# Low parts of the weights: ScalarE's negated high part and an adding DMA from GpSimd, in place of a VectorE subtraction

## The chip, the cores and the metric
The kernel runs on one core of one Trainium2 chip. The metric is the device time of one execution in microseconds (us). The engines have short names in the profile: PE is TensorE (PEld its weight loads), DVE VectorE, ACT ScalarE, POOL GpSimd, and SP the engine that issues DMAs and computes nothing.

## What is computed
One layer of a hybrid decoder, for a prompt of 2048 positions and for 8 sample positions that share the weights:

```
shift, scale, gate = split(silu(c) @ w_ada + b_ada)
h    = x * (1 + scale) + shift
u_s, z_s, q, k, v, z_a, g_s, g_a = split(h @ w_in)
b_s  = (GLU(gelu(SSM(u_s)), w_glu) * silu(z_s)) @ w_branch_s
b_a  = (attention(q, k, v) * silu(z_a)) @ w_branch_a
m    = sigmoid(g_s) * b_s + sigmoid(g_a) * b_a
y    = layer_norm(alpha * x + gate * (m @ w_out))
```

The model width is 1024, all data are float32, and the states and the K/V caches are outputs too.

## The kernel before
**Products from three parts.** The matrix products run in the type float32r, which holds fewer bits than float32. So each operand is split into a high part (the value rounded to float32r) and a low part (value minus high part), and a product is the sum of three: high by high, low of the activations by high of the weights, and high by low of the weights. chunk_k (L75 to L78) issues the three for one slice k of 128 rows; whi and wlo are the two parts of a weight, hh and hl (later xh and xl) those of the activations. chunk (L65) does the 8 slices into one PSUM tile acc (3 buffers), and products (L80) goes over jobs: a job is one weight of 1024 x 128, used for 5 chunks of positions (512, 256, 512, 264 and 512 columns), each with an evacuation evac of its own behind it.

**Where a weight comes from.** split_w (L49 to L60) loads it into the tile wst (one buffer, SP's queue, L55), ScalarE rounds it to whi (L58), and VectorE subtracts to wlo (L59). whi and wlo have two buffers each, so the next weight's parts can be written when TensorE has finished the weight before the present one. products calls split_w for the next weight after the second chunk of the present one; but the order on each engine is made by a scheduler, which puts every instruction where its own model of the times has it, and is then fixed. An engine takes its instructions strictly in that order. 74 weights pass through split_w; w_out and the V projection have code of their own.

**The stages.** At the start (phase_in, L108) the weights of the modulation are loaded and multiplied (ada, L183 to L191), the activations are transposed (L228), scaled to hh (ScalarE, L235) and split to hl (L240: VectorE, and GpSimd for three slices of eight), and the first two weights are split, whose first chunk fills TensorE between the modulation matmuls. Then come the products of w_in, first beside the preparation of the state-space tables, then beside the state-space pairs (ssm_pairs, L684; about 335 to 920 us), in which GpSimd makes small pieces: dg (L763), which VectorE adds into kt (L768), and copies into S (L799 to L806). Attention runs beside further products of w_in (to about 1495 us). Phase 4 has the GLU product (about 1585 to 1780 us), branch a and branch s. In the GLU stage each chunk's evacuation (L1187 to L1196) loads a stored chunk z, ScalarE takes its sigmoid zs and the sigmoid sg of acc, GpSimd multiplies zs by z (L1192) and adds the two parts of the activations into z (L1193), VectorE multiplies twice (L1194, L1195), and SP stores. Last is the product with w_out and the layer norm.

Of the kernel before, what the change touches and what calls it, by code (L numbers as in the profile page):

```python
# [9 lines left out]
F32 = mybir.dt.float32  # L10
F32R = mybir.dt.float32r
I32 = mybir.dt.int32
AF = mybir.ActivationFunctionType
OP = mybir.AluOpType
# [25 lines left out]
class Trunk:  # L40
# [8 lines left out]
    def split_w(self, parts, st=None):  # L49

        nc = self.nc
        if st is None:
            st = self.wp.tile([128, KT, 128], F32, name="wst", bufs=1)
        for src, dst in parts:
            nc.sync.dma_start(dst(st), src)  # L55
        hi = self.wp.tile([128, KT, 128], F32R, name="whi")
        lo = self.wp.tile([128, KT, 128], F32R, name="wlo")
        nc.scalar.copy(hi, st)  # L58
        nc.vector.tensor_tensor(lo, st, hi, op=OP.subtract)  # L59
        return hi, lo  # L60

    def cols(self, w, c0):
# [1333 lines left out]
```

## Time and profile before
| what | value |
|---|---|
| time of the runs shown | 2338.59 us, median of 2 (2336.45 and 2340.74) |
| the profiled execution | 2341.11 us, of which the span of the trace is 2339.3 us |
| busy: PE, DVE, ACT, POOL | 2274.6, 1393.7, 755.1, 329.1 us |
| granted TensorE clock, mean | 0.995 of full speed |
| DMA queue of SP | 388,576 packets, 315.8 MB, 47% of what 16 DMA engines could be busy |
| HBM read and written | 195.3 MB and 122.6 MB |

Busy times are sums over the span; an engine can be busy for little and still be waited for. Every DMA of this kernel is issued by SP. The end of a matmul is modelled, since matmuls are pipelined: the distance from one start to the next tells more than a duration.

### The profile page before, as it was taken

The page shows a single profiled execution, that of the slowest core. Times are in us where ns is not written, and L with a number is a line of the kernel's source. Part 1 is how long each engine was busy: PE and PEld are TensorE (multiplying, and loading weights), DVE is VectorE, ACT ScalarE, POOL GpSimd, SP SyncE. Part 2 cuts the span into 40 slices and gives each one's busy share as a digit, 9 for nine tenths or more (in the row PEclk, how much of TensorE's full clock was granted, in tenths as well). Part 3 has the DMA queues.
Part 4 walks back from the last instruction along what each step waited for, and adds up shares of the span by engine and source line. Part 5 has one row for each costly group of instructions (what it writes and reads, how often), then busy time and mean ns, then how long its engine had stood idle before and what let it go on. Part 6 is the DMA issues. An engine that isn't in the chain of part 4 may idle for free. (4 is left out here: it accounts for less than half of the span.)

```text
span 2339.3 us, 35133 instructions
## 1 busy us (share of the span) xinstructions
PE 2274.6 (97%) x12819; PEld 1903.5 (81%) x12819; DVE 1393.7 (60%) x3100; ACT 755.1 (32%) x1636; POOL 329.1 (14%) x412
## 2 busy tenths in 40 slices
PE   7999999999999999899999999999998999999998
PEld 5888898788888888677888888887877888888886
DVE  4896229888888872067776666426436214224887
ACT  3411213331111211166665565435224113212100
POOL 1100001111101100000010000013542000222232
PEclk9999999999999999999999999999999999999999
DMA  9344623344434445443343333448337546767431
GB/s 290 101 150 127 209 69 112 111 117 119 120 111 121 115 110 127 93 131 111 110 137 96 108 100 114 108 114 221 112 104 231 154 124 198 218 179 230 150 120 65
DMA packets 388749, 318.02 MB, mean 136 GB/s; under 512 B 90582, under 2 KB 332654, under 8 KB 386991
## 3 DMA queue, kind: packets, MB, share of 16 engines
q1 hardware_dynamic: 388576, 315.78, 47.0%
q8 instruction: 101, 1.65, 0.3%
q14 instruction: 72, 0.59, 0.1%
HBM read 195.28 MB, written 122.63 MB: 136 GB/s over the span
## 5 line engine op out<-in xcount | busy, mean ns | idle before, releaser
L78 PE MATMUL acc<-hh,whi 128*128 128x512 f32 (+2 forms) x2000 | 714.0, 358 | 11.2 <-ACT zr L582 10.7
L78 PE MATMUL acc<-hl,whi 128*128 128x512 f32 (+2 forms) x2000 | 706.7, 353 | 0.0
L78 PE MATMUL acc<-hh,wlo 128*128 128x512 f32 (+2 forms) x2000 | 703.2, 352 | 0.0
L78 PEld LDWEIGHTS acc<-hh,whi 128*128 128x128 f32 x2000 | 378.3, 189 | 64.8 <-ACT zr L582 11.1
L78 PEld LDWEIGHTS acc<-hl,whi 128*128 128x128 f32 x2000 | 378.6, 189 | 53.1 <-issue 7.6
L78 PEld LDWEIGHTS acc<-hh,wlo 128*128 128x128 f32 x2000 | 378.1, 189 | 53.1 <-issue 6.9
L78 PE MATMUL acc<-xh,whi 128*128 128x512 f32 (+2 forms) x960 | 336.5, 351 | 15.1 <-ACT sg L1190 13.3
L78 PE MATMUL acc<-xl,whi 128*128 128x512 f32 (+2 forms) x960 | 335.5, 349 | 3.0 <-DVE xl L1138 2.9
L78 PE MATMUL acc<-xh,wlo 128*128 128x512 f32 (+2 forms) x960 | 333.7, 348 | 0.0
L78 PEld LDWEIGHTS acc<-xh,whi 128*128 128x128 f32 x960 | 181.5, 189 | 43.5 <-ACT sg L1190 17.8
L78 PEld LDWEIGHTS acc<-xl,whi 128*128 128x128 f32 x960 | 181.7, 189 | 27.7 <-DVE xl L1138 5.4
L78 PEld LDWEIGHTS acc<-xh,wlo 128*128 128x128 f32 x960 | 181.5, 189 | 23.0
L1138 DVE TENSOR_TENSOR xl<-xst,xh 128x1024 fp32r<-128x1024 f32 (+2 forms) x84 | 105.7, 1275 | 81.0 <-ACT xh L1137 80.0
L59 DVE TENSOR_TENSOR wlo<-wst,whi 128x1024 fp32r<-128x1024 f32 x74 | 95.6, 1292 | 93.0 <-ACT whi L58 92.3
L1035 DVE SCALAR_TENSOR_TENSOR t<-ps,bias 128x512 f32<-128x512 f32 (+1 forms) x128 | 82.7, 671 | 97.7 <-PE ps L1033 96.4
L872 ACT ACTIVATE t<-t,nm 128x256 f32<-128x256 f32 (+1 forms) x256 | 125.5, 492 | 45.2 <-DVE es L869 29.1
L58 ACT CAST whi<-wst 128x1024 fp32r<-128x1024 f32 x74 | 77.6, 1049 | 149.2 <-PE acc L78 146.2
L1137 ACT CAST xh<-xst 128x1024 fp32r<-128x1024 f32 (+2 forms) x84 | 86.0, 1043 | 106.7 <-DMA xst<-mD 34.1
L1068 POOL TENSOR_TENSOR o<-o,z 128x512 f32<-128x512 f32 x32 | 42.6, 1330 | 548.3 <-ACT o L1067 533.2
L582 ACT COPY zr<-acc 128x512 f32<-128x512 f32 (+2 forms) x120 | 60.0, 500 | 168.0 <-PE acc L78 70.5
L1330 PE MATMUL po<-wol,xh 128*128 128x512 f32 (+1 forms) x272 | 102.8, 378 | 0.8 <-DVE wol L1253 0.8
L1330 PE MATMUL po<-woh,xh 128*128 128x512 f32 (+1 forms) x272 | 102.8, 378 | 0.1
(354 smaller groups left out, 3259.8 us busy)
## 6 DMA issues: line engine op xcount, KB each, us to landing
wst<-in_w_in SPq DMA_DIRECT2D x50, 512.0 KB
uD<-u SPq DMA_DIRECT2D x8, 1088.0 KB
u<-uD SPq DMA_DIRECT2D x32, 272.0 KB
yD<-y SPq DMA_DIRECT2D x64, 132.0 KB
x<-in_x_prompt SPq DMA_DIRECT2D x16, 512.0 KB
wa<-in_w_ada SPq DMA_DIRECT2D x16, 512.0 KB
qf<-qD SPq DMA_DIRECT2D x32, 256.0 KB
z<-zaP SPq DMA_DIRECT2D x32, 256.0 KB
```

The costliest lines, as they stand in the source:

```text
L58: nc.scalar.copy(hi, st)
L59: nc.vector.tensor_tensor(lo, st, hi, op=OP.subtract)
L78: self.nc.tensor.matmul(ps[:, :n], w[:, k, :], x[:, k, :], start=(k == 0 and i == 0), stop=(k == KT - 1 and i == 2))
L582: nc.scalar.copy(z[:, :n], ps[:, :n])
L872: nc.scalar.activation(t1[:, h, kw], t1[:, h, kw], AF.Exp, bias=nm[:, h:h + 1], accum_out=den[:, h:h + 1])
L1035: v.scalar_tensor_tensor(t1[:, 2 * g:2 * g + 2, kw], ps[:, :, kw], 0.125, s["bias"][:, hd, b0:b0 + kw.stop], op0=OP.mult, op1=OP.add)
L1068: nc.gpsimd.tensor_tensor(o4, o4, s["z4"], op=OP.mult)
L1137: nc.scalar.copy(xv(hi[:, k - 1:k + 1]), sv(st))
L1138: nc.vector.tensor_tensor(xv(lo[:, k - 1:k + 1]), sv(st), xv(hi[:, k - 1:k + 1]), op=OP.subtract)
L1330: nc.tensor.matmul(ps[:, :w], X[a][:, k, ts], Wo[h * w // 512][b][:, k, ws], start=(i == 0), stop=(i == 23))
```

## The change
One statement of split_w goes and two come. ScalarE writes the negated high part into wlo, and a DMA issued by GpSimd adds the weight, read from HBM once more, to what stands in wlo: st - hi as before, computed as -hi + st.

```diff
         nc.scalar.copy(hi, st)
-        nc.vector.tensor_tensor(lo, st, hi, op=OP.subtract)
+        nc.scalar.activation(lo, hi.bitcast(F32), AF.Copy, scale=-1.0)
+        for src, dst in parts:
+            nc.gpsimd.dma_start(dst(lo), src, accum_op=OP.add)
         return hi, lo
```

Lines behind L59 stand two further down in the changed kernel (L240 becomes L242, L78 becomes L80). The scheduler orders all engines anew. Three places follow.

GpSimd at the start, before: the subtractions for hl of the first chunks stand one behind the other.

```order
L240 TENSOR_TENSOR hl_197<-h,hh_196 128x512 x3
L240 TENSOR_TENSOR hl_506<-h,hh_505 128x256 x3
L240 TENSOR_TENSOR hl_621<-h,hh_620 128x512 x3
L240 TENSOR_TENSOR hl_729<-h,hh_728 128x256 x3
L240 TENSOR_TENSOR hl_833<-h,hh_832 128x512 x3
```

The same place now (L61 is the adding DMA):

```order
L242 TENSOR_TENSOR hl_197<-h,hh_196 128x512
L61 DMA wlo<-in_w_in 128x8x128 x2
L242 TENSOR_TENSOR hl_197<-h,hh_196 128x512 x2
L242 TENSOR_TENSOR hl_508<-h,hh_507 128x256 x3
L242 TENSOR_TENSOR hl_623<-h,hh_622 128x512 x3
L242 TENSOR_TENSOR hl_731<-h,hh_730 128x256 x3
```

The DMAs for the first two weights stand between the first and the second hl of the first chunk.

TensorE at the start, before (pm is the modulation's sum, md and x are transposed, acc the product of the first weights):

```order
L78 MATMUL acc<-hh_196,whi 128x512
L188 MATMUL tr<-ident,md 128x128
L183 MATMUL pm<-wa,c_182 32x128
L78 MATMUL acc<-hl_197,whi 128x512
L78 MATMUL acc<-hh_196,wlo 128x512
L183 MATMUL pm<-wa,c_182 32x128 x15
L228 MATMUL tr<-ident,x 128x128 x4
L78 MATMUL acc<-hh_196,whi 128x512
L188 MATMUL tr<-ident,md 128x128
L183 MATMUL pm<-wa,c_182 32x128
```

TensorE now, from the last modulation matmuls on:

```order
L185 MATMUL pm<-wa,c_182 32x128 x16
L190 MATMUL tr<-ident,md 128x128
L185 MATMUL pm<-wa,c_182 32x128 x16
L190 MATMUL tr<-ident,md 128x128
L230 MATMUL tr<-ident,x 128x128 x6
L80 MATMUL acc<-hh_507,whi 128x256
L230 MATMUL tr<-ident,x 128x128 x6
L80 MATMUL acc<-hh_196,wlo 128x512
L80 MATMUL acc<-hh_196,whi 128x512
L80 MATMUL acc<-hl_197,whi 128x512
```

The first matmul that reads wlo stood among the modulation matmuls and now stands behind the last of them. Before that last one, 30 large matmuls (10 of them on wlo) stand in the order of before, and 4 (none on wlo) in that of the change.

GpSimd in the GLU stage, before, over one change of weight (zs and z of the chunks of 264, 512, 512 and 256 columns):

```order
L1192 TENSOR_TENSOR zs_17003<-zs_17003,z_17001 128x264
L1193 TENSOR_TENSOR z_17001<-xh4_16052,xl4_16053 128x264
L1192 TENSOR_TENSOR zs_17039<-zs_17039,z_17037 128x512
L1193 TENSOR_TENSOR z_17037<-xh2_16002,xl2_16003 128x512
L1192 TENSOR_TENSOR zs_17075<-zs_17075,z_17073 128x512
L1193 TENSOR_TENSOR z_17073<-xh0_15700,xl0_15701 128x512
L1192 TENSOR_TENSOR zs_17111<-zs_17111,z_17109 128x256
```

GpSimd in the GLU stage now, from the chunk of 256 columns on:

```order
L1194 TENSOR_TENSOR zs_16980<-zs_16980,z_16978 128x256
L1195 TENSOR_TENSOR z_16978<-xh3_15996,xl3_15997 128x256
L61 DMA wlo_16992<-in_w_glu 128x8x128
L1194 TENSOR_TENSOR zs_17023<-zs_17023,z_17021 128x512
L1195 TENSOR_TENSOR z_17021<-xh1_15946,xl1_15947 128x512
L1194 TENSOR_TENSOR zs_17059<-zs_17059,z_17057 128x264
```

The sequence of zs and z is the old one; one DMA stands in it per weight, behind the z of the 256-column chunk.

## Rows read from the trace of the kernel before

**Rows 1.** The page's part 1: busy us, share of the span, instructions.
```profile
PE 2274.6 (97%) x12819; PEld 1903.5 (81%) x12819; DVE 1393.7 (60%) x3100; ACT 755.1 (32%) x1636; POOL 329.1 (14%) x412
```

**Rows 2.** Windows: stretch, its us, each engine's busy us, PEclk, DMA share, GB/s.
```profile
20.00:47.00 27.00, 22.07 (x253) 14.54 (x252) 11.41 (x34) 8.48 (x16) 2.12 (x2) 1.00 1.17 301
47.00:100.00 53.00, 52.03 (x326) 43.98 (x325) 45.15 (x135) 33.37 (x61) 14.93 (x15) 1.00 0.42 140
...
335.00:920.00 585.00, 578.24 (x3099) 486.05 (x3098) 469.57 (x990) 132.88 (x239) 69.78 (x186) 1.00 0.41 116
...
1585.00:1780.00 195.00, 183.78 (x966) 155.04 (x965) 97.12 (x106) 71.33 (x108) 87.17 (x73) 1.00 0.52 147
```

**Rows 3.** Waits of TensorE: for whom, us in total, times, longest.
```profile
PE acc L78 <- ACT sg L1190: 13.3, 15, 3.6
```

**Rows 4.** Timeline, ScalarE and TensorE, branch a: start, us, engine line op.
```profile
1852.95 1.06 ACT L58 CAST whi<-wst 128x1024 fp32r<-128x1024 f32 x1
...
1875.33 0.39 PE L78 MATMUL acc<-xl,whi 128*128 128x512 f32 x1
1875.56 0.39 PE L78 MATMUL acc<-xh,wlo 128*128 128x512 f32 x1
```

**Rows 5.** Timeline, ScalarE, GpSimd and TensorE, GLU stage, one weight.
```profile
1662.18 1.03 ACT L58 CAST whi<-wst 128x1024 fp32r<-128x1024 f32 x1
1663.12 1.26 ACT L1190 ACTIVATE sg<-acc,bglu 128x512 f32<-128x512 f32 x2
...
1664.46 1.06 POOL L1193 TENSOR_TENSOR z<-xh,xl 128x256 f32<-128x256 f32 x1
1673.21 1.29 POOL L1192 TENSOR_TENSOR zs<-zs,z 128x512 f32<-128x512 f32 x1 [7.69 <-ACT zs L1191]
...
1680.53 0.39 PE L78 MATMUL acc<-xh,wlo 128*128 128x512 f32 x1
```

**Rows 6.** Groups by line: shapes, count, busy us, mean ns, idle before.
```profile
L59 DVE TENSOR_TENSOR wlo<-wst,whi 128x1024 fp32r<-128x1024 f32 x74 | 95.6, 1292 | 93.0 <-ACT whi L58 92.3
L58 ACT CAST whi<-wst 128x1024 fp32r<-128x1024 f32 x74 | 77.6, 1049 | 149.2 <-PE acc L78 146.2
```

**Rows 7.** Chain that ended last, GLU stage: start, us, what.
```profile
1664.85 0.74 DVE wlo L59
...
1665.73 0.80 issue
1666.53 0.41 DVE z L1194
...
1667.94 4.48 DMA z<-zsD
...
1675.18 3.43 DMA z<-zsD
```

**Rows 8.** Groups by line and form, GpSimd: its shortest frequent instruction.
```profile
L800 POOL MEMSET S<- 128x2 f32 x32 | 3.3, 104 | 0.2
```

**Rows 9.** Timeline of SP, ScalarE and GpSimd at the start.
```profile
19.62 1.05 ACT L58 CAST whi<-wst 128x1024 fp32r<-128x1024 f32 x1 [1.00 <-DMA wst<-in_w_in]
...
21.30 1.74 SPq L55 DMA_DIRECT2D wst<-in_w_in  x1
29.25 1.05 ACT L58 CAST whi<-wst 128x1024 fp32r<-128x1024 f32 x1 [1.70 <-DMA wst<-in_w_in]
34.04 1.29 POOL L240 TENSOR_TENSOR hl<-h,hh 128x512 fp32r<-128x512 f32 x1 [13.21 <-DVE h L239]
```

**Rows 10.** Timeline of GpSimd, state-space stage: dg of two pairs.
```profile
587.08 0.49 POOL L763 TENSOR_TENSOR dg<-ident,dT 16x16 f32<-16x16 f32 x2 [0.74 <-DVE kt L768]
...
603.60 0.49 POOL L763 TENSOR_TENSOR dg<-ident,dT 16x16 f32<-16x16 f32 x2 [4.00 <-DVE kt L768]
```

**Rows 11.** Timeline of VectorE, GLU stage: z without and with GpSimd beside.
```profile
1682.40 0.69 DVE L1194 TENSOR_TENSOR z<-z,zs 128x512 f32<-128x512 f32 x1 [1.18 <-POOL z L1193]
...
1688.44 1.20 DVE L1194 TENSOR_TENSOR z<-z,zs 128x512 f32<-128x512 f32 x1 [5.00 <-POOL z L1193]
```

## The prediction

> **What bounds the kernel now.** I read the busy times first: TensorE is busy 97% of the span and VectorE 60%, ScalarE 32%, GpSimd 14% [rows 1]. Then the same by stage: TensorE is idle 4.9 us of 27 at the start, 6.8 of 585 in the state-space stage, 11.2 of 195 in the GLU stage [rows 2]. All idle time of TensorE together is 2339.3 - 2274.6 = 64.7 us, 2.8% of the span; whatever VectorE is spared, no more than this can be had, and a 2% gain (46.8 us, about what a measurement of this kernel can tell from no change) would need most of it. The waits of TensorE say who could give it back: the longest is for sg of ScalarE, 13.3 us in 15 times [rows 3], and no line names wlo at all. So the subtraction at L59 is nowhere waited for by TensorE directly, and the question is what the new way of making wlo costs, and whether that stays hidden.
>
> **How much cover there is.** A low part is made early. In branch a the cast for one weight starts at 1852.95, and TensorE reads the first wlo of that weight at 1875.56, 22.6 us later; a matmul of 512 columns starts every 0.23 us there [rows 4]. In the GLU stage the cast starts at 1662.18 and the first read is at 1680.53: 18.4 us [rows 5]. At the very start there is hardly any: the first weight's cast starts at 19.62 [rows 9], and the order has its wlo read right behind the first two large matmuls.
>
> **The change, part by part.**
> 1. Removed: 74 subtractions, 95.6 us of VectorE at a mean of 1.29 us [rows 6]. Nothing of it is on TensorE's path but in the GLU stage, where the chain that ended last goes through it: 0.74 us of wlo and 0.80 us of issue behind it before VectorE takes z [rows 7]. GpSimd has given that z free at 1664.46 + 1.06 = 1665.52 [rows 5], so VectorE could start it 1.0 us before 1666.53. The link is there for some 6 weights: -6 us.
> 2. Added on ScalarE: 74 passes over 128x1024. The trace has no such pass; the cast of the same size takes 1.05 us [rows 6], and I take that: 78 us. Bounds: nothing, and twice the cast. ScalarE is busy 32%, and after its cast in the GLU stage it stands idle till the next z lands [rows 5]; I cost it at 0. It shortens the cover by 1.05 us for the pass and up to 0.6 us for the sigmoid that now stands between the two.
> 3. Added on GpSimd: 74 DMAs of 512 KB that add to SBUF. No row of before has a DMA from GpSimd; every one is SP's. Two things have to be priced: how long GpSimd is held by issuing one (P), and when it lands. Bounds of P: below, nothing (SP is held 1.74 us by the same load at the start [rows 9]); above, the shortest GpSimd instruction, 0.104 us [rows 8], for each of the 1024 runs of 512 bytes (128 partitions by 8), 106 us; for each of 128 partitions it is 13.3 us. I take P = 8 us: it is what the same 512 KB took from SP's issue to the cast at the busiest moment, 29.25 - 21.30 = 7.95 us [rows 9], and between the ends that I can name this row is nearest in kind. For landing I take 4 us more (a z load of 256 KB takes 3.43 to 4.48 us [rows 7]). P + 4 = 12 us against 22.6 - 2.1 = 20.5 us in the branches and 18.4 - 2.7 = 15.7 in the GLU stage: hidden in both. The cover is gone at P = 16.5 and P = 11.7.
> The Trainium skill gives a price of its own, "DMA: Bandwidth & Descriptors", section "Anatomy of one DMA — SWDGE (gpsimd) path": about 2.0 us plus bytes over 436 GB/s, for this size 3.2 us (an estimate from the page, for a plain copy). By that the sum below would lose its GLU overrun only; no run so far shows it.
> 4. What is queued behind the new wait on GpSimd. It takes its instructions in order, and each L61 waits for ScalarE's negation. State-space stage: behind it stand dg and the copies into S. dg is made at 587.08 for a kt that lets the next dg go at 603.60 [rows 10], so GpSimd may be some 15 us late there: hidden at P = 8. GLU stage: L61 stands after the z of the 256-column chunk and before the next zs. In that place GpSimd is free from 1665.52 to 1673.21, 7.69 us [rows 5], so P = 8 overruns by 0.3 us; 8 weights: +2 us. From there on each further us of P falls on the chain.
> 5. The bytes. The GLU chain waits for z loads, 4.48 us beside a weight load and 3.43 us without [rows 7]: some 1.05 us per 512 KB in the way. An adding DMA reads HBM and SBUF, so up to twice that; I take 1.5 us x 8 weights = +12 us (bounds 0 and 17). In the state-space stage the DMA share is 0.41 [rows 2], and room is left.
> 6. The start. There the transfers set the pace: DMA share 1.17 at 301 GB/s from 20 to 47 us [rows 2]. Two more weights come by: 1.05 MB at 301 GB/s is 3.5 us, and 7.0 if the second reading counts in full; I take 5. And the order changes: before, 30 of the large matmuls of chunk 0 stand among the modulation matmuls, while these wait for their loads; now only 4 do, and all that read wlo stand behind the last of them. 26 x 0.23 = 6.0 us of work leaves time in which TensorE idled and goes to a stretch where it is full (52.03 of 53 us [rows 2]). +11 us.
> 7. wst comes free after the cast and not after the subtraction, so SP, which waits there in line with the z loads of the GLU stage behind it, issues 1 to 2 us sooner; its next cast comes a whole weight later, 22.6 us in branch a, against some 8 us for a load, so nothing waits for that load and I cost it at 0. Waits in the state-space stage that I can't place: +2.
> Sum: -6 + 2 + 12 + 11 + 2 = +21 us on the profiled execution's 2341.1 us (span 2339.3 and 1.8 around it): 2362. That execution is 2.5 us over the median shown, 2338.6, so on the median's footing 2360 us.
>
> **Rivals.**
> A. GpSimd makes the transfers slowly (ends on the other side). One mechanism: P is long, and in the GLU stage everything over the 7.69 us of free time lands on the chain, 8 times. At P = 16 that is 8 x 8.3 = 66 us in place of 2; the start loses 4 more, since two such DMAs stand ahead of the hl that GpSimd did at 34.04 [rows 9] and finish at 22 + 32 = 54. 2360 + 64 + 4 = 2428. From P = 11 on the loss is over 2% (8 x 3.3 = 26 on top of 21). At P = 20 the branches and the first stage come in as well, some 26 weights x 3.5 us, and 2500 is passed. For it: nothing in the trace says that a GpSimd DMA is quick, and GpSimd takes 1.29 us for 128x512 numbers [rows 9]. GpSimd and VectorE also get in each other's way: the same z takes VectorE 0.69 us alone and 1.20 us beside GpSimd [rows 11]. Were GpSimd's issuing slowed in that ratio, P = 8 becomes 14.
> The Trainium skill has that as a rule, "SBUF — State Buffer", section "SBUF: two separate sides": while VectorE runs certain operations, GpSimd cannot write the descriptors of its DMAs. Its rows here are the two above, which show the conflict between computing instructions only. Against A: 8 us is already 4 times what one reading of 512 KB needs at 301 GB/s.
> B. Nothing to be seen: P of 5 or less, and the added bytes find room. Then the GLU terms are -6 + 0, the start +6: 2338.6. For it: idle DMA time in nearly every stage. Against it: the start, whose order is fixed.
> C. The relief of VectorE is worth over 2%: it would take most of the 64.7 us; the rows give 13.3 us of sg waits, part of which hangs on VectorE. 2290 at best; nothing in the waits bears it out.
>
> **How the numbers follow.** Forecast (2345 to 2385): 0.43. A: 0.37. B (2325 to 2345): 0.17. C: 0.03. Within 2% (2292 to 2385) are the forecast and B less what slips over the edge, 0.59; slower 0.38; faster 0.03. The range leaves out about one in ten on each side: from 2336, inside B, to 2450, P of some 18 in A.
>
> **What would show it.** Right: a GpSimd DMA holds it 5 to 10 us; no wait of TensorE for wlo after the first two weights; the first large matmuls on wlo at about 52 and the stage ends 11 us later; z loads in the GLU stage near 5 us; VectorE's busy time down by 96 us and ScalarE's up by 78. Wrong: waits of zs or z on GpSimd's DMA in the GLU stage, TensorE waiting for wlo in the branches (P over 16), VectorE's instructions in the state-space stage lengthened, or a TensorE clock below full in stages where it was 1.00.

## The result, and the profile after

| | before | after |
|---|---|---|
| time, median of 2 runs, us | 2338.59 | 2407.06 (2405.82 to 2408.29) |
| ratio to before | | 1.0289, 95% interval 1.0272 to 1.0306 |
| span of the profiled execution, us | 2339.3 | 2403.8 |

The changed kernel is slower by 2.9%. That is 47 us beyond the forecast of 2360 and outside the 2345 to 2385 that the forecast was given; it lies inside the outer range (2336 to 2450), in the part that was rival A's. Lines behind L59 have moved by two: L59 is now ScalarE's negation, L61 GpSimd's transfer, the sigmoids L1190 and L1191 are L1192 and L1193.

The page's part 1 of after, to be read against [rows 1]:

```profile
PE 2299.7 (96%) x12819; PEld 1922.4 (80%) x12819; DVE 1310.6 (55%) x3026; ACT 827.0 (34%) x1710; POOL 425.7 (18%) x486
```

VectorE lost 83 us of work, ScalarE gained 72. TensorE has the same 12819 instructions and is busy 25 us longer, with a mean granted clock of 0.978 in place of 0.995: some of its work ran at the lower clock. The groups of the two new lines (the second for the GLU weights), and GpSimd's longest wait:

```profile
L59 ACT ACTIVATE wlo<-whi 128x1024 fp32r<-128x1024 f32 x74 | 78.4, 1059 | 0.4
L61 POOL DMA_DIRECT2D wlo<-in_w_glu x8 | 12.5, 1565 | 29.5 <-ACT wlo L59 29.2 <-issue 0.2
```
```profile
POOL wlo L61 <- ACT wlo L59: 629.6, 55, 43.4
```

The pass costs 1.06 us, as taken. A transfer holds GpSimd 1.57 us, not 8, and the page has its landing a median of 7.8 to 9.0 us after issue, by weight group. The 629.6 us that GpSimd stands in line do not reach TensorE by way of wlo: it waits for that 0.2 us in all. Its waits in after (for whom, us in total, times, longest), to [rows 3]:

```profile
PE acc L80 <- ACT sg L1192: 25.0, 7, 6.0
PE acc L80 <- ACT zr L584: 19.9, 2, 15.4
PE pm L185 <- DMA wa<-in_w_ada: 11.3, 9, 3.4
PE acc L80 <- ACT xh L1139: 8.4, 5, 2.7
```

The wait for sg went from 13.3 us in 15 times to 25.0 in 7: fewer, and up to 6 us long. Windows of after, with the columns of [rows 2]; the last two are a part of the start and one burst of matmuls in the GLU stage:

```profile
20.00:47.00 27.00, 16.98 (x186) 11.15 (x187) 7.99 (x26) 9.68 (x16) 5.28 (x4) 0.76 1.24 268
47.00:100.00 53.00, 49.28 (x312) 40.81 (x306) 35.57 (x82) 28.33 (x52) 14.15 (x13) 0.86 0.41 140
335.00:920.00 585.00, 573.95 (x3114) 482.63 (x3113) 446.20 (x962) 150.59 (x259) 80.69 (x189) 1.00 0.53 128
47.00:60.00 13.00, 9.84 (x64) 6.36 (x58) 7.76 (x19) 5.83 (x13) 2.73 (x3) 0.50 1.02 367
1713.40:1716.70 3.30, 3.30 (x18) 3.30 (x17) 1.84 (x3) 0.00 (x0) 1.87 (x2) 0.50 0.36 114
```

Where the time went is told best by TensorE's lag: the start of the first product with a weight's wlo in one run, less the start of the same one in before, both from the timeline. It grows where time is lost and stays flat elsewhere.

| lag in us at the | start's end (3rd weight, 100 us in before) | end of the state-space stage (31st, 898) | begin of attention's main part (35th, 1030) | end of attention (51st, 1586) | GLU's end (60th, 1809) | branch s (68th, 1990) |
|---|---|---|---|---|---|---|
| after | 16.4 | 25.5 | 33.1 | 35.0 | 60.5 | 64.0 |
| e1_start | -0.5 | 10.0 | 17.0 | 18.9 | 41.8 | 47.0 |
| e2_neg | 1.7 | 5.4 | 0.1 | 4.5 | 16.4 | 16.6 |
| e3_bytes | 4.0 | 6.1 | 3.5 | 3.5 | 14.3 | 12.4 |
| e4_pin | 15.6 | 31.0 | 37.6 | 39.6 | 52.9 | 57.8 |
| e5_late | 0.2 | 2.7 | 2.8 | 2.8 | 21.6 | 22.0 |
| e6_hold | 15.3 | 24.1 | 32.3 | 33.1 | 58.3 | 62.0 |
| e7_all3 | -0.6 | 5.8 | 13.4 | 14.2 | 30.5 | 32.7 |
| e8_plain | 3.2 | 3.6 | 2.6 | 2.6 | 13.5 | 12.6 |
| e9_latepin | -0.5 | -1.1 | -2.1 | -2.1 | -3.8 | -5.4 |
| e10_lolast | 12.8 | 20.5 | 28.0 | 29.9 | 56.6 | 61.6 |
| e11_branch | -0.4 | 0.3 | -0.6 | -0.6 | -1.7 | 0.5 |
| e12_places | 0.2 | 7.8 | 9.1 | 9.7 | 17.5 | 16.8 |
| e13_turn | -0.3 | 1.6 | 0.6 | 0.6 | 5.4 | 4.7 |
| e14_lolast_before | 1.9 | 2.1 | -0.5 | -0.5 | -0.2 | 0.1 |

After loses 16.4 us at the start, 9.1 in the state-space stage, 9.5 up to the end of attention (7.6 of them at once, from 923 to 1030), 25.5 in the GLU stage with its turns (a turn is the last weights of a stage, beside which the next stage's activations are loaded), 3.5 at the turn to branch s, and nothing in the branches: 64.0 of the 64.5 us by which the span grew. Each run has one trace, and where nothing was changed the lag still moves by 2 to 3 us (e3 from 6.1 to 3.5, e14 from 2.1 to -0.5), so a single step of that size shows little.

A part of the loss is the lower clock and not waiting. The same 1082 matmuls of the GLU stage with its turns, in before and in after:

```profile
1585.60:1809.20 223.60, 207.62 (x1082) 175.11 (x1081) 115.52 (x126) 85.82 (x129) 90.11 (x74) 0.99 0.56 165
1620.60:1869.70 249.10, 217.67 (x1082) 186.24 (x1081) 100.64 (x117) 93.93 (x137) 102.19 (x83) 0.92 0.68 168
```

Of the 25.5 us, 10.1 are longer busy time at a clock of 0.92, and 15.4 more idle time. At the start 8.3 of the 16.4 us are longer busy time (92.44 against 84.13 us).

Two things stand out in the GLU stage. The first is ScalarE's order. Its timeline in after, one weight:

```profile
1700.23 1.04 ACT L58 CAST whi<-wst 128x1024 fp32r<-128x1024 f32 x1
1701.16 0.68 ACT L1192 ACTIVATE sg<-acc,bglu 128x512 f32<-128x512 f32 x1
1701.75 1.05 ACT L59 ACTIVATE wlo<-whi 128x1024 fp32r<-128x1024 f32 x1
1711.67 0.63 ACT L1193 ACTIVATE zs<-z 128x512 f32<-128x512 f32 x1 [8.88 <-DMA z<-zsD]
1712.21 1.03 ACT L1192 ACTIVATE sg<-acc,bglu 128x512 f32<-128x512 f32 x2
```

In [rows 5] the cast is followed by both sigmoids of the accumulator (1663.12, x2) before ScalarE takes up a zs. Now the negation stands where the second one stood, and the second sigmoid has come behind a zs that waits 8.88 us for its z load. TensorE, and SP with the next store and z load behind it, wait for that sigmoid:

```profile
1712.93 0.39 PE L80 MATMUL acc<-xh,whi 128*128 128x264 f32 x1 [4.10 <-ACT sg L1192]
```
```profile
1705.04 0.42 SPq L1170 DMA_DIRECT2D z<-zsD  x1
1714.24 0.32 SPq L1198 DMA_DIRECT2D ysD<-sg  x1
1714.61 0.42 SPq L1170 DMA_DIRECT2D z<-zsD  x1
```

The second is the z load itself, from the chain that ended last: 6.56 us beside a weight load and a transfer from GpSimd, where [rows 7] has 4.48 beside a weight load alone.

```profile
1705.04 6.56 DMA z<-zsD
1716.80 3.38 DMA z<-zsD
```

### The profile page after: what moved, and what is told of

Read it like the earlier page. It is cut to its first block, busy times and chain, and to the rows that moved or that the text cites. A ratio compares the mean times of both kernels' runs of the same rounds, so it can differ in the third digit from the quotient of the medians.

```text
span 2403.8 us, 35248 instructions
## 1 busy us (share of the span) xinstructions
PE 2299.7 (96%) x12819; PEld 1922.4 (80%) x12819; DVE 1310.6 (55%) x3026; ACT 827.0 (34%) x1710; POOL 425.7 (18%) x486
## 4 chain that ended last, share of the span: by engine, by line
PE 68%; DMA 13%; DVE 7%; SPq 5%; issue 3%; ACT 2%; POOL 2%; POOLq 0%; DVEq 0%; ACTq 0%
PE acc L80 46%; PE po L1332 7%; PE po L1062 3%; DMA z<-zsD 3%; PE ps L1035 3%; PE pt L1049 2%; DMA tD<-kt 2%; PE acc L663 2%; SPq L178 1%; DMA zsD<-zr 1%; PE yp L815 1%; PE xp L782 1%; PE yp L814 1%; DVE sg L1197 1%; DMA xst<-ozP 1%
## 5 line engine op out<-in xcount | busy, mean ns | idle before, releaser
L80 PE MATMUL acc<-hh,whi 128*128 128x512 f32 (+2 forms) x2000 | 715.9, 358 | 21.8 <-ACT zr L584 19.9
L80 PE MATMUL acc<-hl,whi 128*128 128x512 f32 (+2 forms) x2000 | 707.6, 354 | 0.0
L80 PE MATMUL acc<-hh,wlo 128*128 128x512 f32 (+2 forms) x2000 | 704.5, 352 | 0.0
L80 PEld LDWEIGHTS acc<-hh,whi 128*128 128x128 f32 x2000 | 379.4, 190 | 76.6 <-ACT zr L584 20.4
L80 PEld LDWEIGHTS acc<-hh,wlo 128*128 128x128 f32 x2000 | 379.0, 190 | 53.8 <-issue 7.0
L80 PEld LDWEIGHTS acc<-hl,whi 128*128 128x128 f32 x2000 | 379.3, 190 | 52.2 <-issue 7.1
L80 PE MATMUL acc<-xh,whi 128*128 128x512 f32 (+2 forms) x960 | 341.7, 357 | 33.5 <-ACT sg L1192 25.0
L80 PE MATMUL acc<-xl,whi 128*128 128x512 f32 (+2 forms) x960 | 340.8, 356 | 0.9 <-DVE xl L1140 0.8
L80 PE MATMUL acc<-xh,wlo 128*128 128x512 f32 (+2 forms) x960 | 339.1, 354 | 0.2 <-DMA wlo<-in_w_glu 0.2
L80 PEld LDWEIGHTS acc<-xh,whi 128*128 128x128 f32 x960 | 187.2, 195 | 61.1 <-ACT sg L1192 28.2
L80 PEld LDWEIGHTS acc<-xl,whi 128*128 128x128 f32 x960 | 187.7, 196 | 24.9 <-DVE xl L1140 2.2
L80 PEld LDWEIGHTS acc<-xh,wlo 128*128 128x128 f32 x960 | 187.1, 195 | 24.2 <-DMA wlo<-in_w_glu 0.6
L61 POOL DMA_DIRECT2D wlo<-in_w_in x50 | 78.4, 1567 | 472.6 <-ACT wlo L59 445.2
```

Of the source, the lines that this page charges most:

```text
L61: nc.gpsimd.dma_start(dst(lo), src, accum_op=OP.add)
L80: self.nc.tensor.matmul(ps[:, :n], w[:, k, :], x[:, k, :], start=(k == 0 and i == 0), stop=(k == KT - 1 and i == 2))
```

## The experiments

Two theories of the GLU stage, O (ScalarE's order) and B (bytes beside the z loads), and of the start and the middle the same question in other words: is it who waits behind whom, or what is on the DMA engines?

**ScalarE's pass alone (e2_neg).** In place of the transfer:

```
 nc.scalar.activation(lo, hi.bitcast(F32), AF.Copy, scale=-1.0)
+nc.vector.tensor_tensor(lo, st, lo.bitcast(F32), op=OP.add)
```

> ScalarE's negated copy alone: no transfer from GpSimd; VectorE adds the loaded weight to the negated high part, 74 passes of the length of the subtraction. ScalarE's order in the GLU stage is that of the changed kernel (negation, then the sigmoid of z for the next chunk, and only then the sigmoid that empties the accumulator of the 512 chunk before it). Theory O (the GLU loss is that order: the second sigmoid waits for a z load, and so do its ysD and the next z load): the GLU stage loses 10 to 15 us, 2349 to 2354 us. Theory B (the GLU loss is the bytes of the adding transfer beside the z loads): GLU as before, 2337 to 2342 us.

Measured: 2357.19 us, ratio 1.0075 (1.0060 to 1.0090). The GLU stage lost 16.4 - 4.5 = 11.9 us with no transfer at all, as theory O had it. The z load behind the weight load took 4.00 to 4.33 us inside the stage, no longer than in before, so nothing of it is bytes. (The time is 3 us above that theory's 2354; the lag at the stage's begin is 4.5.) ScalarE's timeline shows the order at work:

```profile
1694.99 0.68 ACT L1191 ACTIVATE sg<-acc,bglu 128x512 f32<-128x512 f32 x1
1695.57 1.05 ACT L59 ACTIVATE wlo<-whi 128x1024 fp32r<-128x1024 f32 x1
1702.78 0.63 ACT L1192 ACTIVATE zs<-z 128x512 f32<-128x512 f32 x1 [6.16 <-DMA z<-zsD]
1703.31 1.03 ACT L1191 ACTIVATE sg<-acc,bglu 128x512 f32<-128x512 f32 x2
```

**The order put back (e4_pin).** After, in the GLU evacuation; issue_after keeps what stands under it behind the named instruction in the engine's order:

```
+s0 = nc.scalar.activation(sg[:, :n], ...)     # as before, now with a name
+if c == 0: self.sg0 = s0.ins
+if c == 1:
+    with self.tc.issue_after(self.sg0):
+        nc.scalar.activation(zs[:, :n], z[:, :n], AF.Sigmoid)
```

> The changed kernel with one edge of order on ScalarE in the GLU stage: the sigmoid of z for the second 512 chunk is issued behind the sigmoid that empties the first one, as it stood before the change. Theory O: the second sigmoid no longer waits for a z load, two z loads go out together again, and 10 to 15 us come back, 2392 to 2397 us. Theory B: the z loads still take 6.5 us, 2405 to 2409 us.

Measured: 2396.12 us, ratio 1.0240 (1.0222 to 1.0257): 11 us back. GLU now loses 52.9 - 39.6 = 13.3 and not 25.5. ScalarE has its two sigmoids ahead of the wait again:

```profile
1708.12 0.68 ACT L1192 ACTIVATE sg<-acc,bglu 128x512 f32<-128x512 f32 x1
1708.70 1.05 ACT L59 ACTIVATE wlo<-whi 128x1024 fp32r<-128x1024 f32 x1
1709.64 0.68 ACT L1192 ACTIVATE sg<-acc,bglu 128x512 f32<-128x512 f32 x1
1718.07 0.63 ACT L1197 ACTIVATE zs<-z 128x512 f32<-128x512 f32 x1 [7.75 <-DMA z<-zsD]
```

The z loads stayed long (5.73 to 6.64 us in the chain), so the order is worth 12 us by both runs, and 13 us are something else. Most of these lie at the turns: e4's lag grows by 5.5 us from the 51st to the 53rd weight, by 4.0 over the six weights up to the 59th (17.8 in after), and by 3.8 to the 60th.

**The bytes alone (e3_bytes, e8_plain).** Before, with a transfer into a tile that nobody reads:

```
 nc.vector.tensor_tensor(lo, st, hi, op=OP.subtract)
+nc.gpsimd.tensor_copy(scr[:1, 0, :1], hi.bitcast(F32)[:1, 0, :1])
+nc.gpsimd.dma_start(dst(scr), src, accum_op=OP.add)   # e8: without accum_op
```

> VectorE's subtraction kept for all weights, and the adding transfer from GpSimd made as well, into a tile that nobody reads, for the first two weights and for the six weights split inside the GLU products; each is issued once the cast is done. ScalarE's order is that of before. Theory B (bytes beside the z loads): the z load behind it takes 6.5 us and not 4.5, 2 us x 6, and the start loses 5: 2338.6 + 17 = 2356 us. Theory O (order on ScalarE): the bytes fall beside a wait that is there anyway, GLU loses under 4 us; with 5 at the start 2344 us.

> The same kernel as the one with VectorE's subtraction and an unread adding transfer for eight weights, but the transfer copies instead of adding. Theory (an adding transfer takes more of the DMA engines than a copy, since it also reads what it adds to): the z load behind it takes 5.5 us and not 7.3, and the loss halves, 2347 us. Rival (the loss is the 512 KB written, adding or not): 2353 to 2357 us, the z loads as long as beside the adding transfer.

Measured: e3 2355.24 us, 1.0068 (1.0049 to 1.0086); e8 2354.90 us, 1.0083 (1.0061 to 1.0105). In e3 GLU loses 10.8 us for six weights and the start 4.0. The chain has the z loads that stand behind weight load and transfer:

```profile
1674.96 7.25 DMA z<-zsD
...
1700.98 7.71 DMA z<-zsD
```

So theory B is true as well: the z loads get longer by the transfer beside them, with ScalarE's order as it was. Adding or copying makes no difference to the time that these runs can tell. In e8 the z loads behind the transfer took 5.95 to 6.70 us in the chain, between the 5.5 of its theory and the 7.25 and 7.71 of e3, but the time is its rival's. The two transfers differ in everything that the page shows of them (adding: 1.56 us of GpSimd, 8320 packets for eight, landing 9.7 us in the GLU stage; copying: 0.92 us, 1152 packets, 6.5 us). Two cautions, by which the 10.8 us are no clean price of the bytes. The small copy that ties the transfer to the cast takes GpSimd up to 1.18 us. And the unread tile takes one of the three buffers of the tile xst, into which the next activations are loaded, so that SP, with z loads behind, stood in line for the last transfer's landing:

```profile
SPq L1172 <- DMA scr<-in_w_glu: 7.8, 1, 7.8
```

In e3 the lag grows by 4.6 us over the weight where this falls. In e8 SP waits so for 5.6 us, and the lag grows by 0.3.

**An accident that confirms the order (e5_late).** Meant to measure the -6 us that the prediction gave to the subtraction leaving the GLU chain: before, with

```
+with self.tc.issue_after(self.prod):        # the product that feeds ysD, chunk 0
     nc.vector.tensor_tensor(lo, st, hi, op=OP.subtract)
```

> The kernel before, with the subtraction of a GLU weight's low part issued on VectorE behind the products that feed the stores ysD, instead of between the two z products; nothing else moves. This is the gain that the prediction gave to taking the subtraction out of the GLU chain, by itself. Theory (the link of 0.74 + 0.80 us per weight is on the path): 5 to 9 us faster for six weights, 2330 to 2334 us beside 2339. Rival (another link stands beside it: the wait for the z load ends last whether VectorE is 1.5 us earlier or not): 2337 to 2341 us.

Measured: 2356.46 us, ratio 1.0088 (1.0072 to 1.0105), 19 us slower, which neither theory had. The edit touches VectorE alone, yet the order on ScalarE flipped in the same way:

```profile
1695.22 0.68 ACT L1195 ACTIVATE sg<-acc,bglu 128x512 f32<-128x512 f32 x1
1702.12 0.63 ACT L1196 ACTIVATE zs<-z 128x512 f32<-128x512 f32 x1 [6.22 <-DMA z<-zsD]
1702.65 1.03 ACT L1195 ACTIVATE sg<-acc,bglu 128x512 f32<-128x512 f32 x2
```

**The same with the order held (e9_latepin), and only inside the stage (e13_turn).** e9 has the edits of e5 and e4; e13 leaves the stage's first weight out of both, and its last two out of the held order.

> The late subtraction again, now with ScalarE's order held: the kernel before, the GLU weights' subtraction issued on VectorE behind the products that feed ysD, and the sigmoid of z for the second 512 chunk kept behind the sigmoid that empties the first (in the run without that edge the order had flipped as it does in the changed kernel, and it was 19 us slower with no transfer and no pass added). Theory (the subtraction's 0.74 + 0.80 us per weight are on the path): 2330 to 2334 us. Rival (z loads end last with or without it): 2336 to 2341 us. If the 19 us stay with the order held, the order on ScalarE is not the cause and the GLU reading falls.

> The late subtraction with ScalarE's order held, now only from the second GLU weight on, so that the turn into the stage keeps the order it had. In the run that moved all of them TensorE's lag against the kernel before fell by 7.6 us over the six weights inside the stage, but 5.7 us had been lost at the turn ahead of it and 3 at the turn behind it. Theory (the link of the subtraction is worth its 1.3 us a weight, and the turn lost it by another order of its casts): 2329 to 2334 us. Rival (what the weights gain, the turns wait for anyway): 2336 to 2339 us.

Measured: e9 2336.04 us, ratio 0.9987 (0.9978 to 0.9996); e13 2345.64, 1.0025 (1.0014 to 1.0036). With the order held the 19 us are gone, so they were the order. Inside the stage the lag fell by 7.6 us in e9 (0.8 to -6.8 over six weights), and by 5.4 in e13 (2.4 to -3.0 over four): 1.3 us per weight, the size of the link in [rows 7]. But both lose most of it again at the stage's ends. e9's time went by its rival; it is 2 us under before, the only run that is. e13 is 7 us above its rival's range and more above its theory's, and its trace shows why: in the last two weights, where nothing held the order, it flipped again, and the lag went from -3.0 to 5.4 us.

```profile
1761.23 0.68 ACT L1195 ACTIVATE sg<-acc,bglu 128x512 f32<-128x512 f32 x1
1769.16 0.63 ACT L1202 ACTIVATE zs<-z 128x512 f32<-128x512 f32 x1 [7.25 <-DMA z<-zsD]
1769.69 0.67 ACT L1195 ACTIVATE sg<-acc,bglu 128x512 f32<-128x512 f32 x1
```

**The start (e1_start, e10_lolast, e14_lolast_before).** e1 splits the first two weights by VectorE. e10 issues the first chunk's eight products with wlo last; e14 is that edit on before.

```
+own = st is not None                          # e1
+if own:
+    nc.vector.tensor_tensor(lo, st, hi, op=OP.subtract)
+    return hi, lo
```
```
-self.chunk_k(acc1, Ws[1], self.X, prev, k)    # e10, e14; the same for acc, Ws[0]
+self.chunk_k(acc1, Ws[1], self.X, prev, k, (0, 1))
...
+self.chunk_k(A, W, self.X, prev, k, (2,))     # in a loop over k of its own
```

> The new way for 72 weights; the first two, which are loaded among the modulation's weights, are split by VectorE's subtraction as before. In the changed kernel's trace TensorE is 16 us late by the second weight, and the lag grows by 25 us in the GLU stage and by some 20 us elsewhere. Theory (the first two low parts come late, so the large matmuls move behind the modulation loads and TensorE idles early at a lower clock): the 16 us come back, 2407 - 16 = 2391 us, and the stretch from 20 to 47 us has TensorE busy 22 us again. Rival (the start only moves a loss that the later stages would show anyway): 2405 to 2409 us. Every other stage should keep its lag under both.

> The changed kernel; for the first chunk of the first two weights all products with the high part are issued first and the eight with the low part last, so that TensorE has matmuls to put among the modulation's while the low parts are still under way. Theory (the start is lost because what reads the late low part holds up all behind it in TensorE's order, and the clock falls over the idle time): the clock from 20 to 47 us is back at 1.00, 10 to 13 of the 16 us return, 2394 to 2397 us. Rival (the start is lost to the bytes of two more weights): 4 us at most, 2403 to 2408 us.

> The kernel before, no part of the change, with the first chunk's low products issued last for the first two weights. With the same edit on the changed kernel TensorE's lag by the third weight was 12.8 us and not 16.4. Theory (the edit itself costs some 6 us at the start, since eight products of the second weight now stand behind all others of that chunk, and hid what it gave back): 2343 to 2346 us. Rival (the edit is free, so most of the start's loss is neither order nor clock but the transfers): 2336 to 2341 us.

Measured: e1 2394.02 us, 1.0234 (1.0217 to 1.0251); e10 2403.62, 1.0286 (1.0272 to 1.0300); e14 2340.37, 1.0006 (0.9996 to 1.0015). e1 gives the start back whole (lag -0.5) and 13 us of time; later stages keep losing. e10 had TensorE at full clock in most of the start, as its theory had it, and yet only 3.6 us of lag came back; by e14's lag the edit costs 1.9 of its own, and nothing in e14's time. Both times went by the rivals, which put the start's loss down to the transfers. SP has a part of it. Its modulation loads, in after and (second fence) in before:

```profile
22.83 20.89 SPq L178 DMA_DIRECT2D wa<-in_w_ada  x8
```
```profile
23.08 14.89 SPq L176 DMA_DIRECT2D wa<-in_w_ada  x8
```

They end 43.72 - 37.97 = 5.8 us late with two transfers between them. (In e3, whose second transfer went out only at 55.9 us, 2.9 us late.) One reckoning adds 26 x 0.23 = 6.0 us of displaced products, and 4.9 for the 9.84 us of work that ran at half clock from 47 to 60 us: 16.7 us beside the measured 16.4. But no run separates these three. For e10 the same reckoning gives 5.8 + 1.9, and 2.0 for 5.86 us of work at a clock of 0.66 from 30 to 40 us: 9.7 of 12.8. What is shown is that the whole loss comes with the first two weights (e1); its parts are argued.

**The middle (e6_hold, e12_places) and the sum (e7_all3).** e6 makes the negation read the loaded weight; e7 has e1, e4 and e6 together; e12 is e7 with twelve more weights by VectorE.

```
-nc.scalar.activation(lo, hi.bitcast(F32), AF.Copy, scale=-1.0)
+nc.scalar.activation(lo, st, AF.Copy, scale=-1.0)
```
```
+if own or self.nw - 1 in (31, 32, 33, 34, 50, 51, 52, 57, 58, 59, 66, 67):   # e12, counted from 0
```

> The changed kernel with one word altered: the negation reads the loaded weight and not its cast, so the load's buffer comes free after the negation (as it did after the subtraction) and SyncE's order has the store of zr ahead of the next weight load again where the change had put it behind. Theory (the buffer that comes free early puts weight loads ahead of the stores that TensorE waits for): TensorE's wait of 15.4 us near 981 us falls back to 10.7, the 2 us near 177 us go as well, 2396 to 2401 us. Rival (these waits come from the bytes of the adding transfers): 2405 to 2409 us, the waits as they are in the changed kernel.

> Three repairs in one: the first two weights by VectorE, the sigmoids of the GLU stage in their old order, and the negation reading the loaded weight. If the three losses are separate places their gains add: 2407 - 13 - 11 - 8 = 2375 us. If they overlap (a lag caught up in one place is lost at the next wait) 2385 to 2395 us. Neither theory brings it below the kernel before, since the bytes beside the z loads stay: z loads of 5.7 to 6.6 us behind the adding transfer.

> The kernel with the three repairs (2378 us), and twelve more weights by VectorE: those whose transfer falls into the start of the attention stage (four) and into the three turns, where TensorE waits for other loads (eight). Theory (the lag that is left grows only where an adding transfer stands beside transfers that TensorE waits for): 8 us come back near 930 to 1030 us and some 12 in the turns, 2356 to 2360 us, with TensorE's wait near 981 us at 10.7 again. Rival (the loss is spread over the weights, 33 us over 72): 12 weights of 72 give back 6 us, 2372 us.

Measured: e6 2403.75 us, 1.0282 (1.0264 to 1.0300); e7 2378.13, 1.0172 (1.0155 to 1.0189); e12 2357.50, 1.0079 (1.0065 to 1.0093). e6 took away the small wait near 177 us (the lag is 15.3 from the third to the ninth weight; in after it rises from 16.4 to 18.3), but not the long one for zr, 16.0 us; its time can't be told from after's. The three repairs add up: their gains measured one by one (13.0, 10.9 and 3.3 us) give 2380, and e7 has 2378. e12's wait for zr:

```profile
PE acc L85 <- ACT zr L590: 11.5, 1, 11.5
```

With four weights' transfers gone, the wait is near the 10.7 us that it has in before, and from the 31st to the 35th weight the lag grows 1.3 us and not 7.6. In e2, with ScalarE's pass and no transfer, it is 11.3. So that loss is bytes, in a stretch where a 3 MB store of SP is under way and TensorE waits for ScalarE's zr, which waits for its own store; the transfer issued there in after, at 950.81, took 30.0 us to land. At the turns e12's lag grows by 0.7 us (51st to 53rd) and 0.0 (59th to 60th), where e7's grows by 4.4 and 1.9, and the turn to branch s costs nothing any more: those losses come with the turns' own weights. The theory of e12 (few places, 2356 to 2360) stood, the even spread (2372) fell.

**Where nothing is near (e11_branch).** The last 14 weights alone in the new way.

> The new way for the last 14 weights alone (all of branch s, most of branch a), the rest by VectorE as before. There the lag of the changed kernel is flat, but for 3.5 us at the turn to branch s. Theory (where the queues are slack the new way costs nothing, and VectorE's relief of 14 x 1.3 us brings nothing, as no one waits for VectorE): 2337 to 2343 us. Rival (VectorE's relief is worth something where it is free of the other losses): under 2334 us.

Measured: 2343.92 us, ratio 1.0022 (1.0013 to 1.0031). Over the 14 weights the lag goes from -1.7 to 0.5 us, all of it at the turn to branch s; VectorE's relief is worth nothing there. The theory was right in kind, but the time is 1 us above its range, and the 5 us over before are clear of noise. The trace, of one of the faster executions, does not show where they are lost.

## Why the prediction was right or wrong

The direction was right, +21 us against +68, and so was the statement that TensorE would not wait for wlo. The size was not. By place, the forecast had 11 us at the start, 8 in the GLU stage (-6 + 2 + 12) and 2 for the rest; the lag has 16.4, 25.5 and 22.1. That 2407 lies inside the outer range is luck: the range reached so far for rival A, a GpSimd held long, which did not happen. Step by step:

- **Step 2, the pass on ScalarE: "I cost it at 0".** This is the step that failed most: one cause, 12 us (e2, and e4 from the other side). The duration was right (1.06 us), and that ScalarE is idle 8 us till the next z was right too. But a new instruction was priced by the room for its duration, and what it cost came from where it stands: it pushed the second sigmoid behind an instruction that waits for a load. The prediction reckoned the new order on TensorE and on GpSimd and left out ScalarE's.
- **Step 3, P = 8 us and landing in 12.** GpSimd is held 1.57 us. The row taken (a load at the busiest moment) was an elapsed time and not an issuing time, where SP's 1.74 us in [rows 9] was the near one. Landing came out at medians of 7.8 to 9.0, single ones at 6.2 to 30.0. By the Trainium skill's fit for one DMA on this path ("DMA: Bandwidth & Descriptors", "Anatomy of one DMA — SWDGE (gpsimd) path") 512 KB would take some 3.2 us, an estimate from that fit. No run here has such a transfer without others beside it; among them a plain copy took 6.5 us (e8), an adding one 9.7 (e3).
- **Rival A** named the right side and the wrong mechanism: it needed P of 11 or more. By the rule of the Trainium skill beside it ("SBUF — State Buffer", "SBUF: two separate sides") GpSimd cannot write the descriptors of its DMAs while VectorE runs certain operations. All 74 transfers hold GpSimd 1.54 to 1.71 us, also the 12 that have a VectorE copy or an operation with a scalar beside them, so the holds show no sign of it; whether a part of the landings is that, no run tells.
- **Step 4**, the overrun of GpSimd in the GLU stage (+2), is nothing at this P.
- **Step 5, bytes: +12 in the GLU stage.** The mechanism is right: the z load beside a transfer takes 2 us more (6.56 against 4.48; 1.5 was taken). That the stage loses 13.3 with the order held is near 12 in part by luck, since 9 of the 13.3 lie at the turns. "Room is left" and the 2 us for what could not be placed missed the most in sum, 22 us in place of 2: 7.6 at one wait for a store behind the state-space stage (e12), 3.5 at the turn to branch s, 1.9 in attention, and 9.1 that stay open. A mean DMA share of 0.41 [rows 2] says nothing of the 30 us in which a single store is waited for.
- **Step 6, the start: +11, measured 16.4.** The bytes' term was right (5 against 5.8 us); the 6.0 of displaced products was not measured by itself. Missing was the clock, which the prediction named only as a sign of being wrong: TensorE, which had waited for its loads, was at 0.50 from 47 to 60 us, where before has 1.00, and 8.3 of the 16.4 us are longer busy time.
- **Step 1, the gain of 6 us** from the link of 0.74 + 0.80 us is real inside the stage (1.3 us per weight in e9 and e13), and mostly given back at its ends.
- **Step 7, wst free earlier, cost 0:** 2 us at one weight (e6), and too little to show in the time.

What stays open: the state-space stage's 9.1 us. Runs that split the weights the new way there show 6 (e7) to 15 us (e4), and even runs with nothing changed there (e5, e13) some 2. It was not tried by itself. Open too are the shares of order, bytes and clock at the start.

## What to carry to other kernels

Where a scheduler sets each engine's order, price a new instruction by what changes places around it, on every engine that the waiting engine waits for: here 1.06 us on an engine idle two thirds of the time cost 12 us, and an edit on VectorE alone flipped ScalarE's order for 19. An edge that pins the order is cheap, and tells at once whether a loss is order or work. Moving work to the DMA engines was near free here only where no short transfer that someone waits for stood beside it, and that is read at those waits and not from the mean share.

## What the hardware showed that was not expected

Behind one wait of 4.1 us TensorE ran at half its clock for 3.3 us. After the matmul of 1712.93, shown above, its timeline has:

```profile
1713.62 0.42 PE L80 MATMUL acc<-xl,whi 128*128 128x264 f32 x1
1713.84 0.42 PE L80 MATMUL acc<-xh,wlo 128*128 128x264 f32 x1
...
1717.11 0.28 PE L80 MATMUL acc<-xh,whi 128*128 128x264 f32 x1
1717.23 0.28 PE L80 MATMUL acc<-xl,whi 128*128 128x264 f32 x1
```

The same matmul starts every 0.22 us and then every 0.12, and the window from 1713.4 to 1716.7 has a granted clock of 0.50, 1.2 in place of 2.4 GHz: half of 3.3, some 1.6 us, is lost on top of the wait. In before, TensorE's waits from 1640 to 1780 us are at most 1.67 us long, and the window of that stretch has a clock of 1.00. In that stage the order made few long waits of many short ones, and the clock made them dearer.

An adding transfer of 512 KB breaks into 1040 packets where a copy makes 144, holds GpSimd 1.56 against 0.92 us and lands 3 us later (e3, e8), and yet the kernel's time cannot be told apart.
